# A decoder layer on one core: the attention phase's loads on ScalarE's queue in half rows, early block sums, an FFN pad of 64 columns, and bias bands read from DRAM tables

## The chip, the cores and the metric

The kernel runs on one core of a Trainium2 chip. The metric is the device time of one execution in microseconds, the median of several runs. The core has five instruction streams that meet only at semaphores: PE (TensorE, matrix products; its weight loads are listed as PEld), DVE (VectorE), ACT (ScalarE), POOL (GpSimd) and SP (SyncE, which here only issues DMAs). DMAs can be issued from SP's stream or from ACT's; each stream is worked in its written order, and a DMA issue that waits for a semaphore holds up what stands behind it on its stream.

## The reference, cut to what matters

One layer on x of 2048 x 1024, all in float32:

```
proj = rms_norm(x) @ w_in
o_a  = sliding-window attention, window 128, 4 heads, relative bias, sinks
o_b  = GLU(gelu(S5 state-space model(u)))                    # 512 channels
o_c  = sparse attention, 4 heads: gate0*compressed blocks + gate1*selected blocks
       + gate2*window of 512; relative bias in each
mixed = concat(rms_norm(o_a), rms_norm(o_b), rms_norm(o_c)) * g_out
x  = x + mixed @ w_out
x  = x + relu(rms_norm(x) @ w_up)**2 @ w_down                # 1024 -> 4096 -> 1024
```

A relative bias is a vector over distance; laid out over queries and keys it becomes a band matrix, constant along its diagonals (a Toeplitz matrix).

## The kernel before

Each float32 product is made of three matmuls on a high and a low part (names ending in h and l: `wo_h`, `mh`, `ml`). The high part is a cast on ACT, the low part a subtraction on DVE. Rows are worked in 16 tiles of 128 (tile i stands in the names: `mix14`, `oc15`).

The phases in time: `phase_front` (input projection, state-space model, up to about 404 us), sliding-window attention with GLU and bias bands (to about 653), `phase_mix` (sparse attention and the out projection, to about 1279), `phase_up` and `phase_down` (the FFN).

**Bias bands.** `bias_vectors` writes the bias by distance to DRAM (`r2`, `rs`). `bias_steps` loads for each head a tile in which partition p holds the vector from offset p on (`T`, 128 x 2033, 1 MB), which is the band with its partitions in reverse order. A product with the exchange matrix `c_anti` on PE (`flip`) turns it, and ACT copies the result from PSUM to `b_sel` or `b_cmp`; likewise `Ts` to `b_swa`. That makes 14 flips, each two matmul instructions in the trace.

**Order in the mix.** `phase_mix` is written as tasks (generators) that yield (engine, estimated ns, code). `flow.run` always takes the task that could start first by the estimates, and among equals the one of lowest rank; so ranks and estimates set the order in which instructions stand in each engine's stream. `Ring`s count free buffers, `Event`s tell of finished work; `landing` estimates when a DMA has landed.

For a tile i of the out projection: `tc` loads of the tile's queries and gates; the three branches are added into `oc` on POOL and stored to `oc_d`; `mixed` loads `mix` from `oa_d`, `ob` and `oc_d` (three DMAs); POOL scales by the inverse norms (`r_a`, `r_b` for the first two parts, for the third `nr`, whose sum of squares `sq` comes from ACT); PE turns it (`ptx`, two of 4 transposes), ACT and DVE split it (`mh`, `ml`); `filled` runs 24 matmuls into `pw` for each half n of the 1024 output columns; `added` adds the residual tile `mx` on DVE, and an ACT Square over `pw` gives the row sums. Only after that Square is the PSUM bank `pw` free for the next half. The `xt` ring, two tiles of 128 x 1024, holds the raw rows of w_out (`oraw`), the residual rows (`mx`), and the block sums' operands (`mt`).

**Hand-over to the FFN.** `phase_up` multiplies blocks of the normalised x1 by blocks of w_up in a scheme with seven block products per step, of which four use differences of blocks. For the first eight row tiles `posted` writes the turned rows to `hT`, and then, tied to tiles 7 to 14, loads four blocks (`mt`), takes four differences on POOL and stores them to DRAM (`sums`). `phase_up` loads its factors as `fx` (1 MB each: fx01 to fx03 are blocks of `hT`, fx04 to fx07 are sums), casts them to `fh`, subtracts to `fl`, and takes weights as `ur`, their sums on POOL as `fs`, split into `uh` and `ul`. The first steps of that stand among the last tiles of the mix. `opening` loads and scales w_out; `PAD` is the width of a small tile (`f_g2`) in `phase_up`.

Of the kernel before, what the change touches and what calls it, by code (L numbers as in the profile page):

```python
# [76 lines left out]
def phase_front(tc, C, x, norm1_g, w_in, u_st, pd, rh_a, prm, dkp, dca, consts, extra, x_t):  # L77

    nc = tc.nc
    with ExitStack() as ctx:  # L80
# [99 lines left out]
        for half in range(2):  # L180
# [40 lines left out]
            else:  # L221
# [3 lines left out]
                run(merge(rest, ssm_steps(tc, C, S, u_st, dkp, dca, tp, ps_g, ps_t)))  # L225
# [439 lines left out]
def bias_steps(tc, C, B, pool, tp, ps, rel_bias, r2, rs):  # L665
# [8 lines left out]
    def flip(n, src, dst, name):  # L674
        pf = ps.tile([P, 512], F32, tag="pg", name="bpf" + name)
        nc.tensor.matmul(pf[:, 0:n], C["anti"], src, start=True, stop=True)
        nc.scalar.copy(dst, pf[:, 0:n])

    def swa(h):
        if h == 0:  # L680
            B["Ts"] = tp.tile([P, 4, 256], F32, tag="Ts", name="Ts")
            base = rs[0]
            nc.sync.dma_start(B["Ts"], bass.AP(base.tensor, base.offset, [[1, P], [384, 4], [1, 256]]))
        flip(512, B["Ts"][:, h:h + 2], B["swa"][:, h:h + 2], f"s{h}")

    def nsa(h):
        if h == 0:
            nc.sync.dma_start(B["far"], rel_bias[31:32].to_broadcast([P, 8]))
        T = tp.tile([P, 2033], F32, tag="T", name=f"T{h}")
        base = r2[4 + h]  # L690
# [392 lines left out]
def phase_mix(tc, C, x, gains, B, cmp, w_out, out_norm_g, g2, pd, oa_d, ob, x1, hT, xs, rr, rh, ss_a, ss_b, r_d, oc_d, release):  # L1083
# [4 lines left out]
    with ExitStack() as ctx:  # L1088
# [17 lines left out]
        for t in (kBw[64:96].bitcast(F32), q_lo[0][64:96].bitcast(F32), q_lo[1][64:96].bitcast(F32), slc):  # L1106
# [9 lines left out]
                                     ("qd", 1), ("tc", 1), ("xt", 2), ("mix", 1), ("mh0", 1), ("mh1", 1), ("fill", 1), ("oc", 2))}  # L1116
# [3 lines left out]
        wout = [Event() for _ in range(NK)]  # L1120
# [30 lines left out]
        def opening():  # L1151
# [3 lines left out]
            for k in range(NK):  # L1155
                yield R["xt"]
                box = {}

                def load(k=k):
                    box["r"] = late["fp"].tile([P, D], F32, tag="xt", name=f"oraw{k}", bufs=2)  # L1160
                    nc.sync.dma_start(box["r"], w_out[0, k * P:(k + 1) * P])
                t = yield "SP", 50, load
                landed = Event()
                fire(landed, t + DMA_NS + 2600)
                yield landed
                for n in range(2):
                    sl = slice(512 * n, 512 * n + 512)
                    yield "ACT", 714, lambda: nc.scalar.activation(late["wh"][k][:, sl], box["r"][:, sl], AF.Copy, scale=late["go"][:, k:k + 1])
                    t = yield "DVE", 796, lambda: nc.vector.scalar_tensor_tensor(late["wl"][k][:, sl], box["r"][:, sl], late["go"][:, k:k + 1],
                                                                                 late["wh"][k][:, sl], op0=ALU.mult, op1=ALU.subtract)  # L1170
                put(R["xt"], t)
                fire(wout[k], t)
                if k == 3:
                    yield R["pw"]
                    yield "PE", 60, turn_rows
                    t = yield "DVE", 300, lambda: nc.vector.tensor_copy(late["rb"], late["ptr"])
                    put(R["pw"], t)
# [6 lines left out]
        def front(i):  # L1184
# [1125 lines left out]
```

## Time and profile before

| | us |
|---|---|
| median of three runs | 2544.19 (2543.75 to 2546.55) |
| profiled execution | 2548.41 |
| its span | 2546.6 |
| PE busy | 2440.5 |
| DVE busy | 1771.2 |
| ACT busy | 1325.9 |
| POOL busy | 1021.1 |

The profile shows one execution. "Busy" counts engine work, not DMA issues. A row of the timeline gives start, duration, engine, line, operation, output and inputs, the tile's form, and in square brackets the idle time before it with what ended it. Rows with SPq or ACTq are DMA issues; their duration is that of the issue, not of the transfer. A row of waits gives total, number of times and the longest. Line numbers are those of the kernel before.

### The profile page before, as it was taken

To read this page: it belongs to the slowest core of one execution; us is meant where nothing else is said; L and a number is where in the kernel's file an instruction comes from. 1 tells how busy PE (TensorE), PEld (TensorE's weight loads), DVE (VectorE), ACT (ScalarE), POOL (GpSimd) and SP (SyncE) were. 2 spreads that over 40 slices of the span, in tenths; PEclk is the share of its full clock that TensorE was granted. 3 is DMA by queue.
4 is the path that set the end of the run, shared out by engine and by line. 5 is a ranking of instruction groups with operands and counts; after the bars stand their busy time and mean duration, and the time that the engine had idled before them with its cause. 6 is when DMAs were issued, how large, how long until landed. Compare 5 with 4: busy or idle time off the path is not lost. (4 is left out here: it accounts for less than half of the span.)

```text
span 2546.6 us, 37996 instructions
## 1 busy us (share of the span) xinstructions
PE 2440.5 (96%) x12766; PEld 2071.8 (81%) x12766; DVE 1771.2 (70%) x3496; ACT 1325.9 (52%) x2768; POOL 1021.1 (40%) x1015
## 2 busy tenths in 40 slices
PE   8999998999799999999799999999999999999999
PEld 7799997777578888888578878788887888888887
DVE  7853876754687788888355555755558888888886
ACT  6453546754576667666255554544444444334442
POOL 0000222211243333332646665566555444545447
PEclk9999999999899999999899999999999999999999
DMA  7462335221222122222466667755547534444335
GB/s 234 136 204 83 106 95 169 80 60 42 80 84 84 59 69 75 65 80 77 146 216 186 188 193 220 220 152 153 152 122 262 160 103 125 135 131 132 121 101 196
DMA packets 394867, 337.21 MB, mean 132 GB/s; under 512 B 42758, under 2 KB 357772, under 8 KB 393232
## 3 DMA queue, kind: packets, MB, share of 16 engines
q1 hardware_dynamic: 357488, 308.56, 40.2%
q10 hardware_dynamic: 37184, 26.22, 3.2%
q8 instruction: 101, 1.65, 0.3%
q14 instruction: 94, 0.77, 0.1%
HBM read 220.15 MB, written 114.55 MB: 131 GB/s over the span
## 5 line engine op out<-in xcount | busy, mean ns | idle before, releaser
L1766 ACT CAST v<-vr 128x512 fp32r<-128x512 f32 x224 | 139.4, 624 | 304.7 <-DMA vr<-vd 144.2
L1767 DVE TENSOR_TENSOR v<-vr,v 128x512 fp32r<-128x512 f32 x224 | 233.6, 1051 | 78.8 <-ACT v L1766 78.6
L2099 PE MATMUL pdc<-dw,v 128*128 128x512 f32 x768 | 187.4, 393 | 4.0 <-ACT dw L1766 2.9
L2099 PE MATMUL pdb<-dw,v 128*128 128x512 f32 x768 | 184.7, 389 | 0.0
L2099 PE MATMUL pda<-dw,v 128*128 128x512 f32 x768 | 184.5, 389 | 0.0
L2099 PEld LDWEIGHTS pdc<-dw,v 128*128 128x128 f32 x768 | 145.3, 190 | 35.5 <-ACT dw L1766 3.4
L2099 PEld LDWEIGHTS pdb<-dw,v 128*128 128x128 f32 x768 | 144.5, 188 | 30.1
L2099 PEld LDWEIGHTS pda<-dw,v 128*128 128x128 f32 x768 | 144.1, 188 | 30.0
L546 POOL TENSOR_TENSOR t<-Q,E 128x508 f32<-128x508 f32 x16 | 22.0, 1376 | 362.9 <-ACT Q L526 324.7
L1766 ACT CAST uh<-fs 128x512 fp32r<-128x512 f32 x124 | 76.2, 621 | 157.2 <-PE pub L1920 58.9
L1891 POOL TENSOR_TENSOR fs<-ur,ur 128x512 f32<-128x512 f32 x62 | 87.3, 1408 | 166.6 <-DMA ur<-in_w_up 120.0
L1767 DVE TENSOR_TENSOR ul<-fs,uh 128x512 fp32r<-128x512 f32 x124 | 124.3, 1004 | 35.1 <-ACT uh L1766 34.9
L1767 DVE TENSOR_TENSOR ul<-ur,uh 128x512 fp32r<-128x512 f32 x93 | 93.5, 1007 | 50.1 <-ACT uh L1766 46.8
L1657 PE MATMUL pw<-wo_h,mh 128*128 128x512 f32 x256 | 104.8, 409 | 16.5 <-ACT pw L1673 15.5
L1337 ACT CAST ths<-pps 128x512 fp32r<-128x512 f32 (+1 forms) x144 | 79.0, 563 | 69.8 <-PE pps L1321 62.5
L1936 POOL TENSOR_TENSOR ev<-e,e 128x512 f32<-128x512 f32 x64 | 93.3, 1458 | 49.1 <-issue 24.7
L1920 PE MATMUL puc<-fh,uh 128*128 128x512 f32 x256 | 101.8, 398 | 6.7 <-ACT fh L1766 3.4
L1342 DVE TENSOR_TENSOR tls<-pps,ths 128x512 fp32r<-128x512 f32 (+1 forms) x144 | 92.5, 657 | 21.4 <-ACT ths L1337 20.2
L1920 PE MATMUL pub<-fh,uh 128*128 128x512 f32 x256 | 102.8, 402 | 2.4 <-DVE e L1929 2.4
L1657 PE MATMUL pw<-wo_h,ml 128*128 128x512 f32 x256 | 104.4, 408 | 0.0
L1657 PE MATMUL pw<-wo_l,mh 128*128 128x512 f32 x256 | 104.1, 407 | 0.0
L1920 PE MATMUL pub<-fl,uh 128*128 128x512 f32 x256 | 102.1, 399 | 0.0
(563 smaller groups left out, 7814.7 us busy)
## 6 DMA issues: line engine op xcount, KB each, us to landing
vr<-vd SPq DMA_DIRECT2D x224, 256.0 KB
vd<-ev SPq DMA_DIRECT2D x128, 256.0 KB
ur<-in_w_up SPq DMA_DIRECT2D x124, 256.0 KB
vd<-e ACTq DMA_DIRECT2D x64, 256.0 KB
dr<-in_w_down SPq DMA_DIRECT2D x32, 512.0 KB
x<-in_x SPq DMA_DIRECT2D x16, 512.0 KB
mx<-in_x SPq DMA_DIRECT2D x16, 512.0 KB
x<-mx ACTq DMA_DIRECT2D x16, 512.0 KB
```

Of the source, the lines that this page charges most:

```text
L546: nc.gpsimd.tensor_tensor(t[:, :, :, 0:n], Q[:, :, :, 0:n], e.rearrange("p g j c -> p j g c")[:, :, :, 0:n], op=ALU.mult)
L1337: yield "ACT", cast_ns(n), lambda: nc.scalar.copy(th[:, 0:nb], pt[:, 0:nb])
L1342: t = yield "DVE", sub_ns(n), lambda: nc.vector.tensor_tensor(tl[:, 0:nb], pt[:, 0:nb], th[:, 0:nb], op=ALU.subtract)
L1657: t = yield "PE", mm_ns(512), lambda: nc.tensor.matmul(pw[n], a[half][:, j], b[k][:, sl], start=k == 0 and m == 0, stop=k == NK - 1 and m ...
L1766: nc.scalar.copy(dh, src)
L1767: nc.vector.tensor_tensor(dl, src, dh, op=ALU.subtract)
L1891: nc.gpsimd.tensor_tensor(t, x, y, op=op)
L1920: nc.tensor.matmul(bank[b], w[:, k], h[o][:, k], start=first and k == 0 and n == 0, stop=k == HALF - 1 and n == 2, skip_group_check=True)
L1936: nc.gpsimd.tensor_tensor(tile_("v" + o), x, y, op=op)
L2099: nc.tensor.matmul(bank[b, q], x[:, q, j], y[:, j], start=first and j == 0 and n == 0, stop=j == 1 and n == 2, skip_group_check=True)
```

## The change

The attention phase's loads and stores (`tc`, `oraw`, `mix`, `mx`, `oc_d`) are issued on ACT instead of SP; `hT`, block sums and the FFN's loads stay on SP. The `xt` ring has four tiles of 128 x 512: w_out, residual rows and the x1 stores go in half rows. Each half of w_out is scaled by a task of its own (`weighed`), the turn of the `r_b` rows too (`rows_turned`). For tiles 14 and 15 the second half uses a bank of the `pq` ring. The block sums are tasks of their own (`block_sums`), which may start as soon as the two tiles that they need are in `hT`. The bias bands no longer need a flip: the bias vectors are written 128 times in DRAM with DMAs from DRAM to DRAM (`bias_rows`, tables `r2w` of 4.4 MB and `rsw` of 0.8 MB, during the front phase), and a load with a row step of one less than the table's width reads the band in its right order. `b_sel` gets a load of its own (0.5 MB a head); `b_cmp` is a strided copy on POOL. `PAD` goes from 56 to 64.

```diff
-def bias_steps(tc, C, B, pool, tp, ps, rel_bias, r2, rs):
+def bias_rows(nc, r2, rs, r2w, rsw):
+    return [lambda h=h: nc.sync.dma_start(rsw[h], rs[h:h + 1].to_broadcast([P, 384])) for h in range(4)] + [
+        lambda h=h: nc.sync.dma_start(r2w[h], r2[4 + h:5 + h].to_broadcast([P, 2160])) for h in range(4)]
+def toeplitz(t, h, n, c0, w):
+    base = t[h]
+    return bass.AP(base.tensor, base.offset + P - 1 + c0, [[w - 1, P], [1, n]])
+def bias_steps(tc, C, B, pool, tp, rel_bias, r2w, rsw):
...
-        nc.sync.dma_start(T, bass.AP(base.tensor, base.offset, [[1, P], [1, 2033]]))
-        for j in range(2):
-            flip(512, T[:, 993 + 512 * j:993 + 512 * j + 512], B["sel"][:, h, 512 * j:512 * j + 512], f"{h}{j}")
-        flip(P, T[:, 0:2033:16], B["cmp"][:, h], f"c{h}")
+        nc.sync.dma_start(T, toeplitz(r2w, h, 2033, 0, 2160))
+        nc.sync.dma_start(B["sel"][:, h], toeplitz(r2w, h, 1024, 993, 2160))
+        nc.gpsimd.tensor_scalar(B["cmp"][:, h], T[:, 0:2033:16], 1.0, 1.0, op0=ALU.mult, op1=ALU.mult)
...
-                    box["r"] = late["fp"].tile([P, D], F32, tag="xt", name=f"oraw{k}", bufs=2)
-                    nc.sync.dma_start(box["r"], w_out[0, k * P:(k + 1) * P])
+                    raw = late["fp"].tile([P, 512], F32, tag="xt", name=f"oraw{k}{n}", bufs=4)
+                    t = yield "ACT", 60, lambda: nc.scalar.dma_start(raw, w_out[0, k * P:(k + 1) * P, sl])
+                    spawn(weighed(k, n, raw, sl), 60 + k, t)
...
-                t = yield "SP", 50, lambda: nc.sync.dma_start(oc_d[i * P:i * P + P], S["oc"].rearrange("p h d -> p (h d)"))
+                t = yield "ACT", 60, lambda: nc.scalar.dma_start(oc_d[i * P:i * P + P], S["oc"].rearrange("p h d -> p (h d)"))
...
-                    alt = i == NT - 1 and n
-                    yield R["pt"] if alt else R["pw"]
+                    alt = i >= ENDING and n
+                    yield R["pq"] if alt else R["pw"]
...
+        def loaded(i, rows, xh, landed):
+            for n in range(2):
+                yield R["xt"]
+                xh[n] = late["fp"].tile([P, 512], F32, tag="xt", name=f"mx{i}{n}", bufs=4)
+                t = yield "ACT", 60, lambda: nc.scalar.dma_start(xh[n], x[0, rows, 512 * n:512 * n + 512])
...
+        def block_sums(m, half):
+            yield E[m]["hT"]
+            yield E[m + 4]["hT"]
...
+            for m in range(4):
+                for half in range(2):
+                    spawn(block_sums(m, half), 100 * (m + 4) + 450, 0.0)
...
-PAD = 56
+PAD = 64
```

How the order moves, at the places of which the prediction speaks. On ACT at the end of the mix, before: the Squares of tiles 13 to 15 (`pw` rows), the casts of the turned tiles (`mh`), and the first casts of sums (`fh06`, `fh07`).

```order
L1673 ACTIVATE pw131_15659,xs_15647<-mx13_15590 128x512
L1682 DMA x1_72<-mx13_15590 128x1024
L1608 ACTIVATE sq15_15766,ns_15764<-mix15_15726 128x256
L1673 ACTIVATE pw140_15743,xs_15778<-mx14_15721 128x512
L1624 CAST mh150_15805<-ptx150_15807 128x512
L1673 ACTIVATE pw141_15791,xs_15778<-mx14_15721 128x512
L1682 DMA x1_72<-mx14_15721 128x1024
L1624 CAST mh151_15838<-ptx151_15840 128x512
L1673 ACTIVATE pw150_15860,xs_15913<-mx15_15837 128x512
L1673 ACTIVATE pw151_15865,xs_15913<-mx15_15837 128x512
L1682 DMA x1_72<-mx15_15837 128x1024
L1766 CAST fh06_16055<-fx06_16003 128x2048
```

And after, from the Square of tile 13's first half on:

```order
L1679 ACTIVATE pw130_15689,xs_15734<-mx130_15676 128x512
L1687 DMA x1_72<-mx130_15676 128x512
L1784 CAST fh06_16111<-fx06_16059 128x2048
L1784 CAST fh07_16117<-fx07_16109 128x2048
L1626 CAST mh140_15767<-ptx140_15769 128x512
L1668 DMA mx140_15791<-in_x 128x512
L1668 DMA mx141_15793<-in_x 128x512
L1626 CAST mh141_15788<-ptx141_15790 128x512
L1679 ACTIVATE pw131_15742,xs_15734<-mx131_15678 128x512
L1687 DMA x1_72<-mx131_15678 128x512
L1598 DMA mix15_15806<-oa_d_71 128x256
L1599 DMA mix15_15806<-ob_70 128x512
```

The casts of fx06 and fx07 moved from behind tile 15 to ahead of tile 14's, and the residual rows and `mix15` are now asked for on this stream.

On SP at the same place, before: the last block sums and the loads of fx06 and fx07.

```order
L1638 DMA mx14_15721<-in_x 128x1024
L1715 DMA mt13_15741<-hT_74 128x2x128 x4
L1720 DMA sums_75<-mt13_15741 128x2x128 x4
L1638 DMA mx15_15837<-in_x 128x1024
L1715 DMA mt14_15857<-hT_74 128x2x128 x4
L1720 DMA sums_75<-mt14_15857 128x2x128 x4
L1852 DMA fx06_16003<-sums_75 128x2048
L1852 DMA fx07_16053<-sums_75 128x2048
```

And after:

```order
L1734 DMA sums_75<-mt310_12969 128x2x128 x2
L1734 DMA sums_75<-mt311_13021 128x2x128 x2
L1870 DMA fx01_16057<-hT_74 128x2048
L1870 DMA fx06_16059<-sums_75 128x2048
L1897 DMA ur01511_16065<-in_w_up 128x4x128
L1897 DMA ur01521_16067<-in_w_up 128x4x128
L1897 DMA ur01522_16069<-in_w_up 128x4x128
L1897 DMA ur01512_16071<-in_w_up 128x4x128
L1897 DMA ur01411_16271<-in_w_up 128x4x128
L1897 DMA ur01421_16273<-in_w_up 128x4x128
L1870 DMA fx07_16109<-sums_75 128x2048
```

All block sums now stand ahead of fx01, and fx06 and fx07 ahead of and among the first weight loads.

On SP where sliding-window attention begins, before: the first bias tile and the first loads of queries, keys and values (`ta0`).

```order
L691 DMA T0_4786<-r2_78 128x2033
L770 DMA hnhn_6112<-pb_68 128x16x4
L905 DMA sk_4664<-in_sinks 128x4
L915 DMA ta0_4701<-pa_67 128x384
L916 DMA ta0_4701<-pb_68 128x128
```

And after:

```order
L687 DMA b_swa_4664<-rsw_81 128x256
L691 DMA b_far_4665<-in_rel_bias 128x8
L693 DMA T0_4790<-r2w_80 128x2033
L694 DMA b_sel_4661<-r2w_80 128x1024 x2
L169 DMA pc_69<-po15_c_4620 128x398
L906 DMA sk_4672<-in_sinks 128x4
L916 DMA ta0_4705<-pa_67 128x384
L917 DMA ta0_4705<-pb_68 128x128
```

Two bands of `b_sel` (0.5 MB each) moved in ahead of the first `ta` load.

More of the change, by code (lines that the diff above doesn't have):

```diff
@@ L672, in bias_steps @@
     B["far"] = pool.tile([P, 8], F32, tag="b_far", name="b_far")
[L674 to L677, printed above, removed]
     def swa(h):
[L680 to L684, printed above, removed]
+        nc.sync.dma_start(B["swa"][:, h], toeplitz(rsw, h, 256, 0, 384))
     def nsa(h):
@@ L1179, in landing, with rows_turned @@
+        def rows_turned():
+            yield R["pw"]
+            yield "PE", 60, turn_rows
+            t = yield "DVE", 300, lambda: nc.vector.tensor_copy(late["rb"], late["ptr"])
+            put(R["pw"], t)
+            fire(rows_there, t)
         def landing(t, nbytes):
@@ L1634, in filled @@
             yield R["fill"]
[L1635 removed]
             rows = slice(i * P, i * P + P)
[L1637 to L1640 removed]
+            landed, outs = [Event(), Event()], [Event(), Event()]
+            xh = {}
+            spawn(loaded(i, rows, xh, landed), 100 * i + R_FINISH - 2, 0.0)
+            spawn(posted(i, xh, outs, rows), 100 * i + R_FINISH, 0.0)
             order = [(n, k) for n in range(2) for k in range(NK)]
[L1642 to L1643 removed]
             pw = {}
@@ L1705, in posted, with turns @@
-            put(R["xt"], t + DMA_NS + 1300)
-            m, ks = (i - 7) // 2, slice(2 * ((i - 7) % 2), 2 * ((i - 7) % 2) + 2)
-            if i < 7 or i == NT - 1:
-                return
-            yield E[7]["hT"]
-            yield R["xt"]
-            t = late["fp"].tile([P, 4, 2, P], F32, tag="xt", name=f"mt{i}", bufs=2)
+            yield "POOL", RSQRT_NS + 200, rsq
+            if i >= NT // 2:
+                return
+            for half in range(2):
+                hx = xh[half].rearrange("p (k t) -> p k t", t=P)
+                yield "POOL", 700, lambda: nc.gpsimd.tensor_scalar(xh[half], xh[half], rr[:, i:i + 1], 1.0, op0=ALU.mult, op1=ALU.mult)
+                yield R["pt"]
+                pt = ps_t.tile([P, 4, P], F32, tag="pt", name=f"pth{i}{half}")
+                def turns():
+                    for j in range(4):
+                        nc.tensor.transpose(pt[:, j], hx[:, j], C["ident"])
+                yield "PE", 4 * TURN_NS, turns
+                for j in range(4):
+                    k = 4 * half + j
+                    t = yield "ACT", 380, lambda: nc.scalar.activation(hx[:, j], pt[:, j], AF.Copy, scale=late["g2"][:, k:k + 1])
+                put(R["pt"], t)
+                t = yield "SP", 50, lambda: nc.sync.dma_start(hT[0, i // 4, half, :, :, i % 4], hx)
+                put(R["xt"], t + DMA_NS)
@@ L1713, in load @@
+            fire(ev["hT"], t + DMA_NS)
+        def block_sums(m, half):
+            yield E[m]["hT"]
+            yield E[m + 4]["hT"]
+            t = []
+            for n in range(2):
+                yield R["xt"]
+                t.append(late["fp"].tile([P, 2, 2, P], F32, tag="xt", name=f"mt{m}{half}{n}", bufs=4))
+            t = [t[n // 2][:, n % 2] for n in range(4)]
+            ks = slice(2 * half, 2 * half + 2)
             def load():
                 for n, (b, k) in enumerate(((0, 0), (1, 0), (1, 1), (0, 1))):
-                    nc.sync.dma_start(t[:, n], hT[0, b, k, :, ks, m])
+                    nc.sync.dma_start(t[n], hT[0, b, k, :, ks, m])
@@ L1737, in starts @@
                     fire(E[i]["go"], 0.0)
+            for m in range(4):
+                for half in range(2):
+                    spawn(block_sums(m, half), 100 * (m + 4) + 450, 0.0)
             spawn(opening(), 60, 0.0)
@@ L2220, in trunk @@
             xs = pool("x_s", 1)
-            C["anti"] = xs.tile([P, P], F32, name="c_anti")
-            nc.sync.dma_start(C["anti"], k_anti)
             C["wmask"] = xs.tile([P, P], F32, name="c_wmask")
```

116 lines of the change are left out of this document (45 added, 71 removed).

## The prediction

> **What bounds the kernel now.** The head of the page comes first, then busy time by stretches of the span, then PE's list of waits, then the timeline where the attention phase passes into the FFN's up phase.
>
> ```profile
> span 2546.6 us, 37996 instructions
> PE 2440.5 (96%) x12766; PEld 2071.8 (81%) x12766; DVE 1771.2 (70%) x3496; ACT 1325.9 (52%) x2768; POOL 1021.1 (40%) x1015
> ```
>
> PE is busy 96% of the span, so a change can give at most the other 106 us, apart from matmuls that it removes or speeds up. In the windows the columns are the stretch's length, the busy time of PE, PEld, DVE, ACT and POOL, PE's granted clock, the DMA share and GB/s.
>
> ```profile
> 650.00:700.00 50.00, 35.79 (x196) 29.90 (x197) 40.68 (x144) 31.01 (x94) 13.78 (x17) 0.85 0.30 91
> 750.00:1200.00 450.00, 441.29 (x2910) 389.58 (x2909) 363.05 (x1058) 298.73 (x708) 160.79 (x351) 1.00 0.23 72
> 1250.00:1300.00 50.00, 37.02 (x147) 28.81 (x146) 13.62 (x14) 13.79 (x21) 20.70 (x49) 0.86 0.61 193
> ```
>
> The attention phase, nearly all of what is edited, has three parts. In its middle (750 to 1200) PE lacks only 8.7 of 450 us. At its opening it lacks 14.2 of 50, and at its end 13.0 of 50, at a granted clock of 0.86. PE's waits name both ends:
>
> ```profile
> PE pw L1657 <- ACT pw L1673: 15.5, 5, 6.1
> PE ppc L1321 <- DVE tls L1342: 8.0, 1, 8.0
> ```
>
> The end, by PE's timeline:
>
> ```profile
> 1225.36 0.51 PE L1657 MATMUL pw<-wo_h,mh 128*128 128x512 f32 x1 [2.89 <-ACT pw L1673]
> ...
> 1237.18 0.79 PE L1657 MATMUL pw<-wo_h,mh 128*128 128x512 f32 x1 [6.09 <-ACT pw L1673]
> ...
> 1241.15 0.39 PE L1657 MATMUL pw<-wo_h,mh 128*128 128x512 f32 x1
> ...
> 1246.95 0.50 PE L1657 MATMUL pw<-wo_h,mh 128*128 128x512 f32 x1 [1.29 <-ACT pw L1673]
> ...
> 1252.30 0.39 PE L1657 MATMUL pw<-wo_h,ml 128*128 128x512 f32 x1
> ...
> 1257.71 0.79 PE L1657 MATMUL pw<-wo_h,mh 128*128 128x512 f32 x1 [5.02 <-ACT pw L1673]
> ...
> 1279.49 0.39 PE L1920 MATMUL pua<-fh,uh 128*128 128x512 f32 x1
> ...
> 1284.81 0.50 PE L1920 MATMUL pud<-fh,uh 128*128 128x512 f32 x1 [2.42 <-ACT fh L1766]
> ...
> 1288.74 0.80 PE L1920 MATMUL puc<-fh,uh 128*128 128x512 f32 x1 [3.42 <-ACT fh L1766]
> ```
>
> By the order these are the first matmuls of pw130, pw131, pw140 and pw141 (tile 13 first half, second half, and so on), the up phase's first matmul, and its first ones on fh06 and fh07. A half takes 24 matmuls; pw140's run 0.233 us apart (1246.95 to 1252.30). From 1237.18 to 1241.15 nine starts take 3.97 us where 9 x 0.233 is 2.1: after that gap PE runs slowly and loses 1.9 us more. The duration of 0.79 or 0.80 at 1257.71 and 1288.74 shows the same; after 2.89 and 2.42 it isn't seen. [...] The sum here goes by the rows alone.
>
> **The change at this end (A).** What holds each wait:
>
> ```profile
> 1224.59 0.60 ACT L1673 ACTIVATE pw<-mx 128x512 f32<-128x512 f32 x1 [1.50 <-DVE mx L1672]
> 1224.60 0.33 ACTq L1682 DMA_DIRECT2D x<-mx  x1
> ...
> 1230.78 0.42 ACT L1608 ACTIVATE sq<-mix 128x256 f32<-128x256 f32 x1 [5.46 <-DMA mix<-oc_d]
> ...
> 1236.41 0.60 ACT L1673 ACTIVATE pw<-mx 128x512 f32<-128x512 f32 x1 [1.50 <-issue]
> ...
> 1245.69 0.59 ACT L1624 CAST mh<-ptx 128x512 fp32r<-128x512 f32 x1 [2.17 <-PE ptx L1622]
> 1246.17 0.61 ACT L1673 ACTIVATE pw<-mx 128x512 f32<-128x512 f32 x1
> ```
>
> ```profile
> 1226.49 0.34 SPq L1579 DMA_DIRECT2D oc_d<-oc  x1
> ...
> 1227.85 0.42 SPq L1597 DMA_DIRECT2D mix<-oc_d  x1
> ...
> 1251.50 0.33 SPq L1638 DMA_DIRECT2D mx<-in_x  x1
> ...
> 1278.09 0.81 SPq L1852 DMA_DIRECT2D fx<-sums  x2
> ```
>
> ```profile
> 1256.16 0.69 DVE L1672 TENSOR_TENSOR mx<-mx,pw 128x512 f32<-128x512 f32 x1 [9.16 <-DMA mt<-hT]
> ```
>
> ```profile
> 1227.67 1.30 POOL L1891 TENSOR_TENSOR fs<-ur,fs 128x512 f32<-128x512 f32 x1
> ...
> 1256.74 0.48 POOL L1604 TENSOR_SCALAR mix<-mix,r_a 128x256 f32<-128x256 f32 x1
> ...
> 1260.99 0.48 POOL L1610 TENSOR_SCALAR mix<-mix,nr 128x256 f32<-128x256 f32 x1
> ```
>
> - *pw131 stays late.* It shares one PSUM bank with pw130 and waits for its Square (1236.41). In the new order that Square stands behind seven uh casts, the last of which needs a fourth fs sum of POOL, after four sums of 1.3 us and the rsqrt that stand behind the last oc15 add. From an oc15 that ends at about 1225.2 this comes to 1232.6, the cast to 1233.3, sq14 (its load lands 2.5 us after its issue, as 1227.85+0.42 to 1230.78) is inside that, and the Square ends at 1235.2 with what queues between. pw131 starts at about 1235.9, 1.3 earlier, and its gap still slows PE.
> - *pw140*: the 24 matmuls of pw131 and two turns, then mh141 and the Square, as now: about 1246.2, 0.75 earlier.
> - *pw141 no longer waits.* Now it waits for pw140's Square, and that for an add at 1256.16, 3.6 us after pw140's last matmul, because mx14 is asked for only at 1251.50 on SP, behind block sums (the row names an mt load, issued right behind on the same queue, which the add doesn't read). With two half rows from ACT's queue right behind mh140 the row is there, and pw141 gets a bank of the "pq" ring. It starts at 1251.7 and, at full pace, ends at 1257.2, where it now ends at about 1265.1 (5.02 of wait and 1.9 of slow matmuls go).
> - *pw150*: mix15 is asked for behind pw131's Square (about 1246.3 to 1247.5), lands at 1250.0, POOL's chain takes 4.7 us (1256.74 to 1261.47) from about 1250.1: ready at 1254.8, hidden behind pw141. The turns end at 1258.5, mh 0.59 and ml 0.69 follow, and 48 matmuls of 0.228 from 1259.3 end at 1270.2.
>
> The up phase starts at 1270.2 instead of 1279.49: **A = -9.3 us**, between -4 (if pw131's half and tile 15's chain keep their times and only pw141's bank and add help) and -13 (if pw131's gap closes too).
>
> **The FFN's first blocks (B).** The fx06 and fx07 loads leave SP only at 1278.09, behind the last block sums; their casts:
>
> ```profile
> 1282.86 1.90 ACT L1766 CAST fh<-fx 128x2048 fp32r<-128x2048 f32 x1 [1.69 <-DMA fx<-sums]
> ```
>
> In the new order block sums end before tile 14's end, fx06 goes out next to fx01, and both casts stand before mh140, about 1239. The waits of 2.42 and 3.42 and the slow run behind the second (1.9) go: -7.7. Next late are fx05, fx02, fx04 and fx03, each of which needs a buffer back: fh05 can be cast only behind pw151's Square (about 1271.5), against a need at 1270.2 + 36 x 0.228 = 1278.4, which holds; the fourth is some 1 us late. **B = -6.5**, between -2 and -7.7.
>
> **Bias bands (C).**
>
> ```profile
> L676 PE MATMUL bpf<-T,c_anti x16: 590/592/697, 408.0 to 456.9; 128*128 128x512 f32 x16
> ```
>
> ```profile
> 404.00:425.00 21.00, 16.61 (x62) 10.81 (x61) 14.64 (x35) 13.82 (x36) 6.37 (x6) 0.76 0.73 194
> 425.00:460.00 35.00, 32.38 (x189) 24.79 (x189) 33.09 (x101) 30.78 (x96) 9.99 (x9) 1.00 0.56 167
> ```
>
> ```profile
> 408.02 1.47 POOL L782 TENSOR_TENSOR qda<-ta,rh_a 128x768 f32<-128x768 f32 x1 [6.70 <-DMA ta<-pb]
> ```
>
> Fourteen flips on PE (in 28 instructions) and fourteen copies on ACT go. Up to 425 the flips lie in time in which sliding-window attention waits for its first ta, so they give nothing. Behind it, 12 of the 16 bpf instructions (12 x 0.59 = 7.1) lie where PE is busy 32.4 of 35 us, but DVE 33.1, so half is taken: -3.5. Against it, SP now issues T0 and two sel bands ahead of the first ta, 1 MB more: 1.0 MB at 194 GB/s is 5 us, in which other phases' work still runs; +0.5 is taken. The four cmp copies on POOL (no row of this form; its 128x768 product takes 1.47) lie beside POOL's 25 free us of 35. The table copies, 5.2 MB, run before 400, where PE lives off what it has:
>
> ```profile
> 185.00:400.00 215.00, 212.58 (x1414) 207.26 (x1413) 133.17 (x306) 101.43 (x216) 35.34 (x33) 1.00 0.33 97
> ```
>
> 97 GB/s at a share of 0.33 makes 5.2 MB a further 0.08: nothing. If the weight loads lose that cover, it costs 3. **C = -3**, between -7 and +6.
>
> **The opening (D).** PE's 7.96 us gap is DVE's rsqrt work, which stays ahead of the tls that PE waits for. The 16 w_out loads and casts come earlier and in halves, so out-projection matmuls can fill later gaps: up to the other 6.3 us idle there; but casts put before attention's own can cost the same. **D = 0**, between -4 and +4.
>
> **ACT's queue (E).** Some 160 issues join ACT: 32 tc, 48 mix, 16 oc_d, 16 w_out, 32 x and 16 more x1.
>
> ```profile
> L1596 SPq DMA_DIRECT2D mix<-ob x16: 319/430/766, 675.0 to 1250.3; - x16
> ```
>
> At 0.43 us that is 69 us of its sequencer beside 298.7 of 450 busy. The pair at 1224.59 shows an issue running under an activation, so the issue itself is nearly free. What can cost is a wait at the head of ACT's queue, since casts (ths, mh, Square) stand behind it and PE behind those:
>
> ```profile
> SPq L1579 <- POOL oc L1399: 141.7, 15, 22.2
> SPq L1595 <- PE ptx L1622: 128.6, 11, 28.1
> ```
>
> SP came to these early and had nothing else to do; ACT comes to them later, with rows between. All of it exposed would be +270, none of it 0. In the order an oc_d store stands 3 to 18 ACT rows behind the copy (oTs or oTw) from which its chain starts: a turn on PE, a product on DVE and two adds on POOL,
>
> ```profile
> L1399 POOL TENSOR_TENSOR oc<-oc,ots x32: 722/737/1245, 672.6 to 1217.6; 128x256 f32<-128x256 f32 x32
> ```
>
> some 3.5 us by 2 x 0.74 and two steps near 0.7 with their handovers. Ten rows of about 0.6 cover that. Tiles 5, 6, 12 and 13 have 3 to 5 rows and may wait 1.5 us each, 6 in all; PE has other work queued, so half is taken. The low end is nearest because twelve of sixteen are covered. **E = +3**, between 0 and +15. In sum A to E nothing is gained from a faster transfer. [...]
>
> **Pad (F).** It shifts tiles by 32 bytes and no row of the order: 0. Block sums and hT work only move, under POOL's 290 free us in 750 to 1200.
>
> **Sum:** -9.3 - 6.5 - 3 + 0 + 3 = -15.8. The profiled run took 2548.41 (2546.6 of span and 1.8 around it), 4.2 above the median of the three runs, 2544.19; against that median the forecast is 2528.4.
>
> **Rivals.**
> 1. *Slower: ACT's queue blocks.* Where oc_d's store or a mix load waits at the head of ACT's queue, casts stall and PE with them. It decides from 1.2 us in each of 16 tiles (18.8 / 16 with A, B, C); at the 1.6 that a ninth of SP's 141.7 + 128.6 gives over 16 tiles, +26 instead of +3, the time is 2551. For it: ACT would be at 75 to 80% in the middle. Against: twelve of sixteen stores have their cover. Chance 0.10.
> 2. *The boundary gives half.* oc15 ends no earlier than now, fs sums hold uh and the Squares behind them, pw131 doesn't move, tile 15 waits for its mix: A = -4, B = -3, C = -3, E = +3: 2537. For it: POOL's fs sums of 1.3 us now stand before mix14. Chance 0.17.
> 3. *All of it comes:* A = -13, B = -7.7, C = -7, E = 0: 2516.5. For it: each of these waits is at a named late load. Chance 0.13.
> 4. *It does nothing:* bias loads hold back ta (+6), E = +6, A and B give -11: +1, 2545. Chance 0.10.
>
> The forecast has 0.50. A measurement of this kernel can tell about 0.2%, 5 us, from no change (its three runs spread by 2.8). Faster holds the forecast, rivals 2 and 3: 0.80; within 0.2%: 0.10; slower: 0.10. The range goes from below rival 3 (2512) to half of rival 4 (2543); without rivals 2 to 4 it would be 2519 to 2535.
>
> **What would show it.** Right: the first pua near 1265 to 1270 less what C gives; no ACT wait before pw141 and none for fh at the first pud and puc; block sums gone from SP after tile 14; PE in 425 to 460 with fewer matmuls and the same progress; 750 to 1200 still above 98% busy. Wrong: waits of PE on ths, mh or pw casts in the middle that have an oc_d or mix issue ahead of them on ACT; a late first qda; fh05 or fh04 waits in the up phase; a pw150 that waits for ml.

## The result and the profile after

| | before | changed kernel |
|---|---|---|
| median of four runs (lowest to highest) | 2543.97 us (2543.35 to 2546.55) | 2511.73 us (2509.98 to 2513.25) |
| profiled execution | 2548.41 us | 2512.47 us |
| ratio to before | | 0.9871, interval 0.9854 to 0.9888 |

The change takes 32.2 us off, where 15.8 were forecast (2528.4, range 2512 to 2543): twice as much, and 0.3 us below the range. The head of the changed kernel's page:

```profile
span 2510.4 us, 37968 instructions
PE 2408.8 (96%) x12738; PEld 2064.4 (82%) x12738; DVE 1780.0 (71%) x3496; ACT 1322.1 (53%) x2754; POOL 1037.5 (41%) x1027
```

PE's busy time falls by 31.7 us, almost the whole gain. The 28 flip matmuls that went had 13.4 us of it; most of the rest, 13.7 us, falls in the FFN's up phase, where no matmul went. There matmuls run in less time each (pub's median duration falls from 396 to 389 ns), or waste less at a lowered clock (0.99 granted before, 1.00 after, in the rows below), and a hunt for idle time alone doesn't find that part. The windows of the changed kernel, in the columns of the table shown before, have the up phase as their last row. Its end is taken here, and in all that follows, at the first matmul on `pdc`, which is the 25th of the down phase and starts some 8.5 us behind that phase's first:

```profile
404.00:425.00 21.00, 11.57 (x46) 8.83 (x44) 11.82 (x25) 8.76 (x21) 7.11 (x10) 0.60 0.73 254
425.00:460.00 35.00, 30.58 (x188) 24.12 (x187) 30.68 (x96) 28.37 (x91) 12.60 (x12) 1.00 0.74 206
650.00:700.00 50.00, 39.00 (x195) 34.82 (x196) 42.04 (x124) 36.04 (x102) 17.38 (x25) 0.72 0.37 111
750.00:1200.00 450.00, 440.54 (x2946) 391.77 (x2947) 365.86 (x1067) 303.13 (x708) 164.21 (x348) 1.00 0.25 79
1250.00:1300.00 50.00, 47.94 (x211) 38.67 (x211) 30.73 (x29) 25.82 (x38) 26.50 (x26) 1.00 0.47 145
1262.40:1897.20 634.80, 626.09 (x2776) 516.00 (x2776) 384.96 (x431) 334.13 (x570) 396.93 (x271) 1.00 0.61 179
```

The up phase of the kernel before, between the same two matmuls:

```profile
1279.50:1933.80 654.30, 639.84 (x2778) 518.29 (x2776) 380.88 (x435) 339.44 (x576) 390.34 (x271) 0.99 0.61 180
```

The same 2776 matmuls take 13.7 us less of PE's time, and the phase is 19.5 us shorter. Four points of the trace divide the span (us; in brackets the difference between the two):

| | last GLU matmul | last window-attention matmul | first up matmul | first `pdc` matmul |
|---|---|---|---|---|
| before | 652.8 | 1218.7 | 1279.5 | 1933.8 |
| after | 642.5 (-10.3) | 1206.5 (-12.2) | 1262.4 (-17.1) | 1897.2 (-36.6) |

Sliding-window attention gives 10.3, the middle of the sparse attention 1.9, its end 4.9, the up phase 19.5. The profiled execution before lies 4.4 us above its median and shows nearly all of that in its up phase: five kernels below, with the same slow pace and equally late block sums, have 648.6 to 651.5 instead of 654.3. PE's waits that are left:

```profile
PE pw L1656 <- ACT pw L1679: 10.9, 5, 7.2
PE pqc L1300 <- DVE qB L1228: 8.0, 4, 7.1
PE gpt L611 <- POOL z L608: 5.1, 1, 5.1
```

The waits for `fh` at the start of the up phase are gone, and so is the one before pw141. The pw wait lost a third only. The rsqrt gap at the opening stays (7.1 in place of 8.0, now in front of another matmul), and a new wait of 5.1 us stands in sliding-window attention.

The end of the mix, from PE's timeline after (pw130, pw131, a turn of tile 14, pw140, two turns of tile 15, the first up matmul):

```profile
1211.59 0.50 PE L1656 MATMUL pw<-wo_h,mh 128*128 128x512 f32 x1 [1.29 <-ACT pw L1679]
...
1224.51 0.80 PE L1656 MATMUL pw<-wo_h,mh 128*128 128x512 f32 x1 [7.20 <-ACT pw L1679]
...
1233.15 0.44 PE L1624 MATMUL ptx<-c_ident,mix 128*128 128x128 f32 x2 [0.82 <-POOL mix L1612]
...
1234.89 0.50 PE L1656 MATMUL pw<-wo_h,mh 128*128 128x512 f32 x1 [1.30 <-ACT pw L1679]
...
1247.90 0.44 PE L1624 MATMUL ptx<-c_ident,mix 128*128 128x128 f32 x2 [1.40 <-DVE ml L1627]
...
1249.55 0.44 PE L1624 MATMUL ptx<-c_ident,mix 128*128 128x128 f32 x2 [1.21 <-POOL mix L1612]
...
1262.44 0.50 PE L1938 MATMUL pua<-fh,uh 128*128 128x512 f32 x1 [1.53 <-ACT pw L1679]
```

pw131 waits 7.20 now where it waited 6.09, and its matmul of 0.80 shows the lowered clock behind the gap (0.57 granted from 1224.4 to 1228.0); pw141 runs on behind pw140 without one.

### The profile page after: what moved, and what is told of

Read it like the earlier page. It is cut to its first block, busy times and chain, and to the rows that moved or that the text cites. A ratio compares the mean times of both kernels' runs of the same rounds, so it can differ in the third digit from the quotient of the medians.

```text
span 2510.4 us, 37968 instructions
## 1 busy us (share of the span) xinstructions
PE 2408.8 (96%) x12738; PEld 2064.4 (82%) x12738; DVE 1780.0 (71%) x3496; ACT 1322.1 (53%) x2754; POOL 1037.5 (41%) x1027
## 4 chain that ended last, share of the span: by engine, by line
PE 62%; DVE 3%; DMA 3%; issue 3%; POOL 2%; ACT 2%; ACTq 0%; SPq 0%; DVEq 0%; POOLq 0%
PE pdc L2117 7%; PE pdb L2117 7%; PE pda L2117 7%; PE pub L1938 6%; PE pw L1656 6%; PE puc L1938 6%; PE pua L1938 5%; PE pdd L2117 3%; PE pud L1938 3%; PE pos L1357 2%; PE pps L1324 2%; PE pow L1357 1%; PE pqs L1299 1%; PE pqs L1300 1%; PE ppw L1324 1%
## 5 line engine op out<-in xcount | busy, mean ns | idle before, releaser
L1785 DVE TENSOR_TENSOR ul<-fs,uh 128x512 fp32r<-128x512 f32 x124 | 130.9, 1057 | 32.5 <-ACT uh L1784 31.9
L1785 DVE TENSOR_TENSOR ul<-ur,uh 128x512 fp32r<-128x512 f32 x93 | 99.4, 1071 | 48.2 <-ACT uh L1784 45.5
L1938 PE MATMUL pua<-fh,uh 128*128 128x512 f32 x256 | 99.7, 389 | 1.5 <-ACT pw L1679 1.5
```

What stands on the lines that cost most here:

```text
L1785: nc.vector.tensor_tensor(dl, src, dh, op=ALU.subtract)
L1938: nc.tensor.matmul(bank[b], w[:, k], h[o][:, k], start=first and k == 0 and n == 0, stop=k == HALF - 1 and n == 2, skip_group_check=True)
```

## The experiments

The first theory: the gain beyond the forecast lies in the up phase, where matmuls got faster, so in the pad, which the forecast had set at 0. Its rival: it is the earlier block sums and half rows, and the pad does nothing.

**The pad alone, on the kernel before.**

```diff
-PAD = 56
+PAD = 64
```

> The kernel before with the pad at 64 instead of 56 and nothing else. Theory 1 (address): the pad shifts the factor tiles that stand behind f_g2 (fh and fl of 05, 02, 04, 03) by 32 bytes, and matmuls that read them then start 0.2267 us apart instead of 0.2333; 4 of 7 products x 12 matmuls x 32 steps = 1536, times 6.7 ns = 10 us: ratio about 0.996, median about 2534, and the medians of pua, pub, puc durations go from 394 to 396 ns to 389. Theory 2 (the faster up phase has another cause, e.g. block sums or the x1 rows arriving otherwise): within 1 us of before, durations unchanged.

2537.18 us against 2544.93, ratio 0.9971 (0.9962 to 0.9979): -7.4. No row of any engine's order differs, so the gain lies in the tiles' addresses. The up phase falls to 642.2 us. Groups of matmuls in it, by output, with the shortest, median and longest duration in ns, before:

```profile
L1920 PE MATMUL pub<-fh,uh x256: 389/396/628, 1298.2 to 1924.5; 128*128 128x512 f32 x128
L1920 PE MATMUL pud<-fh,uh x128: 389/389/628, 1284.8 to 1910.6; 128*128 128x512 f32 x128
```

and with the pad of 64:

```profile
L1920 PE MATMUL pub<-fh,uh x256: 389/389/504, 1300.7 to 1915.1; 128*128 128x512 f32 x128
```

What counts is the pace from start to start. From PE's timeline of the kernel before, first matmuls of groups of 12 near the phase's end:

```profile
1875.25 0.40 PE L1920 MATMUL pub<-fh,uh 128*128 128x512 f32 x1
...
1878.06 0.40 PE L1920 MATMUL pua<-fh,uh 128*128 128x512 f32 x1
...
1880.86 0.40 PE L1920 MATMUL puc<-fh,uh 128*128 128x512 f32 x1
...
1889.20 0.39 PE L1920 MATMUL pud<-fh,uh 128*128 128x512 f32 x1
...
1891.92 0.39 PE L1920 MATMUL puc<-fh,uh 128*128 128x512 f32 x1
```

and with the pad of 64:

```profile
1877.73 0.39 PE L1920 MATMUL pua<-fh,uh 128*128 128x512 f32 x1
...
1880.45 0.39 PE L1920 MATMUL pud<-fh,uh 128*128 128x512 f32 x1
...
1883.17 0.39 PE L1920 MATMUL puc<-fh,uh 128*128 128x512 f32 x1
```

Twelve matmuls take 2.80 us or 2.72, which is 233 ns or 227 for one. Before, the slow ones are the products on fh05, fh02, fh04 and fh03, whose tiles lie behind the small tile `f_g2` whose width PAD is; those on fh06 and fh07, in front of it, run at 227. Four products of 32 groups of 12 matmuls, 1536 in all, at 7 ns each, are 10.8 us, somewhat more than the measured 7.4 or the phase's 8.

**The pad taken out of the changed kernel.**

```diff
-PAD = 64
+PAD = 56
```

> The changed kernel with the pad back at 56. Theory 1 (address): 10 us slower than the changed kernel, about 2522 (ratio to before 0.991), with the up matmuls at 392 to 396 ns. Theory 2 (another cause): still 2512.

2515.92 us, 0.9890 (0.9874 to 0.9907), where 2522 was expected: 4.2 above the changed kernel and 1.3 above its second measurement (2514.62, further down). The intervals overlap, so the times alone don't show it; the trace does, with slow medians again (395 for pua, 396 for pub) and an up phase of 641.3 instead of 634.8. So the pad is part of the gain in either kernel.

**Other widths on the kernel before: 48 and 72, then 96 and 128.** Is it the width, more room, or a multiple of an address step?

```diff
-PAD = 56
+PAD = 48    # also 72, 96, 128
```

> The kernel before with the pad at 48 (192 bytes, a multiple of 64 as 256 is). Theory 1 (the address modulo 64 bytes counts): as fast as pad 64, about 10 us under before, up matmuls at 389 ns. Theory 1b (the tiles must be further apart, so a larger pad helps): no gain, 394 to 396 ns.

> The kernel before with the pad at 72 (288 bytes, 32 above a multiple of 64, as 224 is). Theory 1 (address modulo 64 bytes): no gain over before, up matmuls at 394 to 396 ns. Theory 1b (a larger pad helps): as fast as pad 64.

> The kernel before with the pad at 96 (384 bytes, a multiple of 128 but not of 256). 64 gave the faster pace; 48, 56 and 72 didn't, so a multiple of 64 bytes is not enough. Theory A (multiples of 128 bytes): up matmuls at a median of 389 ns, about 8 us under before. Theory B (multiples of 256 bytes): 392 to 396 ns, no gain.

> The kernel before with the pad at 128 (512 bytes). Theories A and B (multiples of 128 or of 256 bytes): 389 ns and about 8 us under before. Theory C (it is no address rule but the one layout that 256 bytes happen to make): 392 to 396 ns, no gain.

One execution each: 2545.31 and 2544.85 (the kernel before beside them 2544.93), and 2540.49 and 2539.15 (2541.57). The up phase took 651.4, 650.8, 649.7 and 647.9 us. At 48 and 96 columns (192 and 384 bytes) the products on the tiles behind the pad have medians of 392 to 395 ns, and 72 (288 bytes) takes as long as before; at 128 (512 bytes) all have 389, as at 64 (256 bytes). The phase of 128 columns is still 5.7 us longer than that of 64, but not by its pace. In these up phases 34 to 61 starts come over 300 ns behind the one before (waits, and slow running behind them). What these lose beyond 227 ns each is 26.4 us at 128 columns and 20.6 at 64. Without that loss the phase takes 621.6 us at both, against 631 to 632 at 48, 56, 72 and 96 columns; in the changed kernel it is 621.2 with 64 and 631.2 with 56. So the pace alone is worth 10 us wherever it was changed, as the 10.8 above say, and what the whole kernel keeps of it varies with its waits. It does not follow the width: 64 and 128 columns are fast, 48, 72 and 96 are not. That leaves the address.

**The small tile moved behind the large ones.** If the address decides, the old width of 56 must give the fast pace too, once nothing large lies behind it.

```diff
-        g2t = pool("f_g", 1).tile([P, PAD], F32, name="f_g2")
         factors(ORDER[3:])
+        g2t = pool("f_g", 1).tile([P, PAD], F32, name="f_g2")
```

> The kernel before with the pad at 56, but the small tile f_g2 stands behind the factor tiles instead of ahead of them. Theory B (what counts is that the factors' addresses, which it shifted, keep to multiples of 256 bytes): the up phase is as fast as with pad 64, matmuls at a median of 389 ns, 5 to 8 us under before. Theory D (it is the distance or the size of the pad itself, not the factors' address): no gain, 392 to 396 ns.

2538.55 us against 2544.09, ratio 0.9980 (0.9970 to 0.9991): -5.1, all medians 389, up phase 644.4 (621.6 without the late starts). That settles the pad: its term is -5 to -7.4 in the kernel before, and it moves the large tiles behind it from a displacement that is slow, 224 bytes, to one that is as fast as none.

**Bias tables alone, on the kernel before.**

```diff
-        dst = flip(512, T[:, 993 + 512 * j:...], B["sel"][:, h, ...])    # PE, then an ACT copy
+        nc.sync.dma_start(B["sel"][:, h], toeplitz(r2w, h, 1024, 993, 2160))
...      # likewise b_swa; b_cmp by a POOL copy out of T
```

> The kernel before with the bias bands read from DRAM tables and nothing else. Forecast in the prediction: -3 us, from half of the flips' PE time less some delay of the first attention loads (ratio 0.999). Rival: all of the flips' time on PE and ACT is on the path of this phase, so the 13.4 us of PE busy time go nearly whole: GLU ends 10 us earlier, ratio 0.996.

2536.19 us against 2541.57, ratio 0.9981 (0.9972 to 0.9990): -4.8, or -5.4 by the medians.

**Tables, with the selected band copied out of T on ACT.** Is the extra 2 MB of loads what holds the gain down?

```diff
-        nc.sync.dma_start(B["sel"][:, h], toeplitz(r2w, h, 1024, 993, 2160))
+        for j in range(2):
+            nc.scalar.copy(B["sel"][:, h, 512*j:512*j+512], T[:, 993+512*j:993+512*j+512])
```

> As the run with the DRAM tables, but the sel band is copied out of T by ACT (8 copies of 128x512) instead of being loaded by a DMA of its own, so 2 MB less are loaded and ACT has 8 of its 14 copies back. If the extra loads hold back the first attention steps: faster than with the loads by up to 5 us. If ACT's copies are what slowed this phase: slower, back towards the kernel before. If only PE's flips count: the same.

2542.11 us, ratio 0.9998 (0.9989 to 1.0007): no gain by the median. Eight copies return, every flip stays away:

```profile
L695 ACT COPY b_sel<-T x8: 607/622/632, 404.5 to 447.3; 128x512 f32<-128x512 f32 x8
```

Eight copies of 0.62 are 5.0 us of ACT, against 5.9 between the two medians. So the extra loads cost less than they save, and taking the flips off PE is not enough. That the gain is ACT's time is likely but not shown: the traced execution, 2538.13 us, is one of the faster ones, and in it sliding-window attention ends at 647.0, between 644.5 with the loads and 648.6 or later with flips. Its ACT also waits 2.8 us for T ahead of the first copy, and its PE 5.6 us for POOL's qda, so the copies' time and the changed order are not separated.

**The changed kernel again, and with flips as before.**

```diff
-            b_swa, b_nsa = bias_steps(tc, C, B, bp, xs, rel_bias, r2w, rsw)
+            b_swa, b_nsa = bias_steps(tc, C, B, bp, xs, ps_x, rel_bias, r2, rs)
```

> The changed kernel as it is, as the measure for the other three of this call: 2511 to 2513, ratio 0.987. If the parts add up, 7 us of it are the pad and 5 the tables, and the three undone parts below share the other 20.

> The changed kernel with the bias bands flipped on PE as before. By the run with the tables alone: 5 us slower than the changed kernel (2517). By the prediction's term: 3 slower. If the later w_out work fills what the flips leave free, nothing.

2514.62 us (ratio 0.9877, 0.9856 to 0.9898) and 2516.27 (0.9890, 0.9874 to 0.9907). The flips cost about 3 in the changed kernel; the intervals overlap, so that alone would not show it, but by the trace sliding-window attention ends at 648.6 with flips and at 637.0 and 642.5 without. All traces of this case agree: 648.6 to 655.5 in the nine with flips, 637.0 to 647.0 in the ten without. A part that the tables lose again, alone (3.9 us) as in the changed kernel (5.1), is a wait of PE for POOL, whose timeline after reads:

```profile
408.77 0.40 POOL L695 TENSOR_SCALAR b_cmp<-T 128x128 f32<-128x128 f32 x1 [7.26 <-DMA T<-r2w]
409.23 1.45 POOL L912 MEMSET qBa<- 64x512 f32 x3
410.76 0.62 POOL L608 TENSOR_SCALAR z<-u_st 128x512 f32<-128x512 f32 x1
```

The copy to b_cmp waits for the 1 MB load of T, and z, for which PE waits 5.1 us, stands behind it on the same stream.

**All loads back on SP's queue, the rest of the change kept.**

```diff
-                t = yield "ACT", 60, lambda: nc.scalar.dma_start(oc_d[i * P:i * P + P], ...)
+                t = yield "SP", 50, lambda: nc.sync.dma_start(oc_d[i * P:i * P + P], ...)
...      # the same for tc, oraw, mix and mx
```

> The changed kernel with tc, w_out, mix, x loads and oc_d stores issued on SP again (half rows, early block sums, the pq bank and the rest stay). By the prediction's terms: the queue move costs 3 us in the middle and brings most of the 9 at the end, so 5 us slower than the changed kernel. Rival 1 (ACT's queue blocks): faster than the changed kernel. Rival 2 (order of issue is all that counts, and half rows and early sums give it on SP as well): within 2 us of the changed kernel.

2508.24 us, ratio 0.9861 (0.9844 to 0.9878), beside 2514.62 of the changed kernel: faster, where 5 us slower was expected. Measured once more, beside another set of runs of the kernel before:

> The changed kernel with the attention's loads back on SP, again, as the measure for the next one: about 2508, 4 us under the changed kernel, ratio 0.986. If the earlier difference was chance, 2512.

2505.08 us, ratio 0.9853 (0.9840 to 0.9867), the best of all, 37 below the kernel before. The mean of its two ratios is 0.9857 and that of the changed kernel 0.9874: ACT's queue costs some 4 us. The single intervals overlap, so this rests on two measurements of each and on the traces. In the middle PE is busy 3.8 us more on SP (444.3 in both runs, beside 440.5 and 440.3), in the row of this kernel:

```profile
750.00:1200.00 450.00, 444.30 (x2960) 393.89 (x2961) 365.44 (x1067) 301.92 (x706) 162.70 (x347) 1.00 0.26 80
```

At the end of the mix (pw131, two turns of tile 14, pw140, tile 15's turns) its PE has:

```profile
1214.13 0.50 PE L1656 MATMUL pw<-wo_h,mh 128*128 128x512 f32 x1 [1.59 <-ACT pw L1679]
...
1221.16 0.44 PE L1624 MATMUL ptx<-c_ident,mix 128*128 128x128 f32 x2 [0.82 <-DVE ml L1627]
...
1225.27 0.69 PE L1624 MATMUL ptx<-c_ident,mix 128*128 128x128 f32 x2 [3.67 <-POOL mix L1612]
...
1227.25 0.80 PE L1656 MATMUL pw<-wo_h,mh 128*128 128x512 f32 x1 [1.30 <-ACT pw L1679]
...
1243.04 0.66 PE L1624 MATMUL ptx<-c_ident,mix 128*128 128x128 f32 x4 [1.40 <-DVE ml L1627]
```

pw131 waits 1.59 instead of 7.20, and the up phase starts without a wait at 1254.5. What changed for pw131 is the order, which follows the estimates. With the loads on SP pw130's add (DVE, 1212.58) and Square (ACT, 1213.36) stand ahead of the uh and ul work of the first steps of the FFN; with the loads on ACT they stand among it (1222.34 and 1223.73), behind casts that wait for POOL's sums. From the last window-attention matmul to the first up matmul it is 49.2 and 48.7 us on SP, 55.9 and 57.2 on ACT, and 60.8 before. On ACT the three loads of mix15 come apart:

```profile
1234.17 0.39 ACTq L1598 DMA_DIRECT2D mix<-oa_d  x1
1234.61 0.47 ACTq L1599 DMA_DIRECT2D mix<-ob  x1
1234.64 0.19 ACT L1679 ACTIVATION_READ_ACCUMULATOR pw<-mx 128x1 f32 x1
1239.87 0.33 ACTq L1600 DMA_DIRECT2D mix<-oc_d  x1
1245.40 0.42 ACT L1610 ACTIVATE sq<-mix 128x256 f32<-128x256 f32 x1 [10.56 <-DMA mix<-oc_d]
```

The third goes out 5.3 us after the second, though its store to oc_d had left at 1213.27. In the trace that issue waits for semaphore 104, which its own load then updates. All 1395 issues of this trace, 1151 of SP and 244 of ACT, name one of eight such semaphores (99 and 101 to 107), each 174 or 175 times. The DMA before it on number 104 is a load of w_up that SP issued at 1236.96, and its last update came at 1239.85, 0.02 us before the issue. The issue holds ACT's stream meanwhile, with sq15 and the Squares of pw140 and pw141 behind it, and this load lands 5.5 us later still, at 1245.38. Earlier in the trace it goes the other way: on number 101, SP issues a load of w_up at 1210.05, 5.2 us after its issue before that had ended and 0.02 us after the last update from a load of mx that ACT had issued at 1206.81. So in these two places the shared semaphore holds the issue; what one of its own would gain was not tried.

**Block sums late again, in the changed kernel.**

```diff
-                    spawn(block_sums(m, half), 100 * (m + 4) + 450, 0.0)
+                    spawn(block_sums((i - 7) // 2, (i - 7) % 2), 100 * i + R_FINISH, t)   # tiles 7 to 14
```

> The changed kernel with each block sum tied to the end of a row tile from 7 to 14 again, as before. By the prediction's term B: fx06 and fx07 are late, the waits at the first pud and puc are back, 6 to 8 us slower than the changed kernel. Rival (early sums collide with the attention's loads in the middle and give as much as they take): the same time.

2522.35 us, ratio 0.9916 (0.9902 to 0.9931): 8 and 11 above the changed kernel's two results. The waits return at the up phase's start, PE's timeline:

```profile
1266.13 0.49 PE L1939 MATMUL pud<-fh,uh 128*128 128x512 f32 x1 [1.35 <-ACT fh L1785]
...
1268.46 0.50 PE L1939 MATMUL pud<-fl,uh 128*128 128x512 f32 x1 [1.83 <-DVE fl L1786]
...
1278.11 0.50 PE L1939 MATMUL pub<-fl,uh 128*128 128x512 f32 x1 [1.82 <-DVE fl L1786]
```

The up phase starts at 1261.9, as in the changed kernel, and takes 644.1 us instead of 634.8 and 631.7. So the early sums are worth some 10, all of it net in the up phase; the waits named make half of it. Ahead of it two effects cancel: with late sums the mix takes 573.8 us from the last GLU to the last window-attention matmul (564.0 and 566.2 with early ones), and its end takes 48.1 (55.9 and 57.2), although the loads are on ACT. So the 7 us at the end are the cost of ACT's queue together with the early sums, not of the queue by itself.

**Half rows alone, on the kernel before's other choices** (flips, pad 56, SP's queue, late sums, a second bank for tile 15 only).

```diff
-                    box["r"] = late["fp"].tile([P, D], F32, tag="xt", name=f"oraw{k}", bufs=2)
+                    raw = late["fp"].tile([P, 512], F32, tag="xt", name=f"oraw{k}{n}", bufs=4)
...      # and w_out's scaling, the residual rows and the x1 stores in halves
```

> Of the change only the half rows are left: the ring of four tiles of 128x512, w_out, x and x1 in halves, w_out scaled by tasks of its own, rows_turned. Flips, pad 56, issue on SP, block sums tied to tiles 7 to 14, and the pq bank for tile 15 alone, are as before or nearly so. By the prediction (D = 0, nothing for half rows by themselves): within 3 us of before. Rival (the ring is what lets the out projection start and run earlier): 8 to 13 us under before, ratio 0.995 to 0.997, and PE's busy time in 700 to 1200 rises by 4 to 7 us.

2530.00 us against 2542.01, ratio 0.9948 (0.9935 to 0.9960): -13.2, the largest single part, at the upper end of what the rival said. Scaling casts of w_out, min/median/max in ns and first to last start, before:

```profile
L1168 ACT ACTIVATE wo_h<-oraw,wo_g x16: 707/721/760, 666.5 to 737.8; 128x512 fp32r<-128x512 f32 x16
```

and with half rows:

```profile
L1168 ACT ACTIVATE wo_h<-oraw,wo_g x16: 705/708/714, 664.3 to 693.0; 128x512 fp32r<-128x512 f32 x16
697.21 0.39 PE L1655 MATMUL pw<-wo_h,mh 128*128 128x512 f32 x1
```

The first out-projection matmul comes at 697.2 (721.3 before), since w_out is ready 45 us earlier. Yet by the last window-attention matmul this kernel is only 4.1 us ahead, 1.8 of which it had when the mix began. From there to the first up matmul it gains 6.2 (54.6 for 60.8): pw131 waits 1.59 in its trace, on SP's queue too, because pw130's add (1220.31) now stands ahead of the ul subtractions and not behind them (1235.65 before, though its residual row had been asked for at 1201.30). pw141 still waits 4.49. The rest, about 3, would be in the up phase, which takes 647.7; with 648.6 to 651.5 in the five kernels with whole rows that is not shown.

**The second bank for tile 15 only, and, on SP, from tile 13 on.**

```diff
-                    alt = i >= ENDING and n
+                    alt = i == NT - 1 and n      # or: i >= ENDING - 1 and n, with the loads on SP
```

> The changed kernel with the pq bank for tile 15 alone, as the one bank swap before was (there in the pt bank). By the prediction's term A (pw141 waits again for pw140's add and Square): 2 to 4 us slower than the changed kernel, with a wait of 1.5 to 3 us at the first matmul of pw141. Rival (pw141's wait came from the late x row alone, which is early now): the same time.

> A version meant to beat both kernels: loads on SP, and the pq bank from tile 13 on. In the changed kernel pw131 waits 7.2 us for pw130's Square; with loads on SP that wait is 1.6 at most. With a bank of its own pw131 waits for nothing: 1.5 to 3 us under the version on SP, ratio 0.985. Rival (PE then waits at ptx140 for POOL's mix14 instead): the same as the version on SP.

2513.84 us, ratio 0.9891 (0.9875 to 0.9906). The ratio is 4 to 5 us above the changed kernel's two, but the intervals overlap and the median lies between the two medians. The trace shows the part: the wait at pw141 is back, and the end of the mix takes 61.8 us instead of 55.9 and 57.2. So tile 14's bank is worth some 4 us.

```profile
1244.40 0.80 PE L1656 MATMUL pw<-wo_h,mh 128*128 128x512 f32 x1 [4.35 <-ACT pw L1679]
```

With tile 13 too, on SP: 2507.03 against 2505.08, 0.9863 (0.9850 to 0.9877): nothing more. The rival was right. pw131 waits for nothing now, and PE waits 5.16 us for tile 14's mix instead (3.67 before):

```profile
1228.42 0.69 PE L1624 MATMUL ptx<-c_ident,mix 128*128 128x128 f32 x2 [5.16 <-POOL mix L1612]
```

## Why the prediction was wrong, step by step

The single parts, each measured by taking it out of the changed kernel or by doing it alone: half rows -13, early sums -10, pad -5 to -7, tables -3 to -5, tile 14's bank -4, ACT's queue +4. They make -31 to -35 where -32.2 was measured. Each is known to 2 to 4 us only, so this says no more than that nothing large is left over. The steps that failed are two parts that the forecast set at nothing: the pad (F), and what half rows do by themselves (D). The others came out within some 5 us of their terms.

- **F, pad: 0 forecast, -5 to -7.4 measured on the kernel before, -1 to -4 by the medians in the changed one. This step failed.** "No row of the order" was taken for "no cost": the pad moved four operand tiles to addresses at which PE runs 3% faster, 10 us of pace in the up phase. The trace before showed it, unread: medians of 396 for pub and 389 for pud at the same shape.
- **A, end of the mix: -9.3 forecast, -4.9 in the changed kernel, -11.6 and -12.1 with its loads on SP.** The mechanism was right: pw141's late row and its bank are what it waited for, and the wait is gone. What carries it is the half-row ring and the bank, and the queue to which the forecast gave a part takes 7 us of it back through pw131 and mix15. That pw131 stays late was right, and for the reason given, its Square behind the uh casts, but only in this order: it waits 7.20 where about 4.8 was forecast, and with the loads on SP 1.59. That mix15 lands 2.5 us behind its issue was wrong: its last part left 5.3 us late and took 5.5.
- **D, opening: 0 forecast. This step failed too, by what it left out.** The rsqrt gap stayed, as written. But half rows are worth -13.2 alone, of which 6.2 belong to A, some 2 are D's, and about 3 remain, for which no term stood and whose place is not shown. Pricing the ring only by its two visible places was the error.
- **B, first FFN blocks: -6.5 forecast, -8 to -11 measured.** Right in its place (no wait for `fh` is left at pud and puc), too small because waits for `fl` and the work behind them go too; its bound of -7.7 was the sum of the waits in one row each.
- **C, bands: -3 forecast, -4.8 alone and about -3 in the changed kernel.** Right in size, in part by luck. The forecast counted PE's flips and no copy on ACT, but with eight copies back and no flip the gain is gone by the median; and the POOL copies, taken as covered, hold z and cost PE a 5.1 us wait.
- **E, ACT's queue: +3 forecast, +4 measured.** Right in size, and the agreement is luck in part. It was placed in the middle alone: 750 to 1200 lost 3.8 us of PE's busy time (97.9% busy, just under the 98% named as a sign) and the end of the mix 7, while sliding-window attention ended some 5 us earlier with ACT's queue than with SP's (637.0 to 642.5 in five traces, 642.7 to 646.8 in three). Rival 1 (ACT's queue blocks) named the right mechanism and was far too large; its +26 also comes from a tenth of SP's 141.7 + 128.6 us, where a ninth is written, which would be +30. The transfers changed little: over the 16 tiles the three loads of mix landed 2.1, 2.9 and 2.7 us after their issue on ACT (medians, changed kernel) and 2.3, 3.1 and 2.9 on SP (kernel before), those of mix15 after 2.5, 2.8 and 5.5 and after 3.4, 3.8 and 3.7. What changed more is the time of issue, at mix15 to a later one: its third load leaves at 1239.87, and at 1230.51 in the second run with the loads on SP.

Rival 3, that all of it comes, was the nearest, and it still lacked F. Rival 2's late tile 15 was there in part (A at -4.9).

Open are four things: why the whole kernel keeps only a part of the 10 us of pace; why the first factor, fh01, which lies in front of the pad, also goes from a mean of 228 to 230 ns to 227; what the up phase gains from half rows; and what it would bring to give mix15's third load a semaphore of its own.

## What to carry to other kernels

Compare the pace of groups with the same shape before predicting that a change of layout does nothing: two medians that differ by 2 or 3% in a phase of 2800 matmuls are worth more than most waits in the list. When a load is late, try smaller pieces and a free buffer on the queue where it stands first; moving the issue to an engine that computes put its wait in front of that engine's work here (5.3 us ahead of sq15), and the version with the loads left on SP is the fastest (2505 us). Price every part of a bundle by the rows it touches, those in the next phase too. Work taken off the bottleneck brings only what the other engines then let it use: ten us of busy time went from PE with the flips, and with eight copies left on ACT the median did not move.

## What the runs showed of the hardware that was not expected

- The pace of the same fp32 matmul of 128x512 depends on where its operand tiles lie in the on-chip buffer: 227 ns from start to start (389 in duration) with a small tile of 256 bytes in front, and 233 ns (392 to 396) on the tiles behind one of 224 bytes. By the durations 192 and 384 bytes are slow too (392 to 395), and 512 bytes or no such tile in front are fast (389); 288 bytes gave no gain in time. Only these widths were run.
- DMA issues of two streams held each other through a shared completion semaphore in the changed kernel: an issue on ACT left 5.3 us after the one ahead of it, with its data stored since 1219.97, at 1239.87, 0.02 us after the last update from a weight load of SP's; and one of SP's left at 1210.05, 0.02 us after the last update from a load that ACT had issued.
